# A PEER block kernel on one core: a new order of the build's steps, gate tiles with their own space, and the last 32 tokens' gates kept in SBUF

## Chip, cores and metric

One core of a Trainium2 chip runs the whole kernel. The metric is device time in microseconds (us) of one execution; lower is better. Engines are named as in the profile: PE is TensorE (its weight loads are PEld), DVE is VectorE, ACT is ScalarE, POOL is GpSimd, SP is SyncE, which here only issues DMAs.

## What is computed

Cut to the second half of the block, which the change touches (512 tokens, 1024 channels, 8 heads, 128 x 128 = 16384 experts, everything float32):

```python
def peer_ffn(h, w_q, sub_keys, expert_u, expert_v):
    q = (hb @ w_q).reshape(tokens, 8, 2, 128)
    s = einsum('thpc,hpkc->thpk', q, sub_keys)
    top_s, top_i = top_k(s, 16)                       # per head, for both halves of the key
    cand_s = top_s[:, :, 0, :, None] + top_s[:, :, 1, None, :]
    cand_i = top_i[:, :, 0, :, None] * 128 + top_i[:, :, 1, None, :]
    fin_s, fin_pos = top_k(cand_s, 16)                # 16 experts per token and head
    idx = take_along_axis(cand_i, fin_pos)
    gates = softmax(fin_s)
    act = gelu(einsum('thkd,td->thk', expert_u[idx], hb))
    return einsum('thk,thkd->td', gates * act, expert_v[idx])
# before it: a pooling and convolution mixer; after it: x + peer_ffn(h), and a final rmsnorm
```

## The kernel before, in words

Each token uses 128 of the 16384 experts. For the first 384 tokens (TD, three blocks of 128) the kernel does not fetch these experts' rows: it runs through all experts in 128 steps of 128 and multiplies with a dense matrix of gates that is zero nearly everywhere. For the last block of 128 tokens it gathers the rows of u and v by indirect DMA. Of the dense tokens the last 64 (TM) have their u products from gathered rows too, so the dense u product covers 320 tokens (TU).

float32 products are made of three matmuls on split operands: a high part (a cast by ACT) and a low part (raw minus high, a subtraction on DVE or POOL).

Stages, in the order of the program, all written out by hand (`manual_schedule`); every engine runs its instructions in that order, and so does each DMA queue:

- The mixer, up to some 290 us.
- **Norm and heads**: the normed tokens are transposed into h2H and h2L (`norm_T`), then for each head the queries, the keys' scores, and the best 16. Between these stand **u steps** (`u_tick`): step i loads a 128-expert block of u (`u_load`, two steps ahead of its cast), casts it (`u_high`, ACT), subtracts (`u_low`), multiplies it with the 320 tokens (`u_mm`, 24 matmuls), and applies Gelu (`u_act`, ACT), whose result is written to DRAM (Ad). n_ahead = 75 such steps are done ahead of the v stage: U_NORM at the norm, U_HEAD in the heads, U_GATE in the gates, 48 in the build, U_END after it.
- **Gates**: softmax, the keys' numbers (`pair_mults`, `pair_keys`), and three columns of 384 tokens (key 0, key 1, gate).
- **Build**: 48 pairs of two groups of four tokens. `one_hots(n)` makes two one-hot matrices oi and oj of 128 x 4 x 128 by compares on DVE; the gate is multiplied in either by four scalings on ACT (even groups) or in four 128-wide instructions on DVE that make oj (odd groups). Eight matmuls a pair set up the dense gate matrix of these tokens in PSUM; ACT copies it to `stage` (`to_stage`), and each 32 tokens' block goes to DRAM (Gd). Each pair also holds one u step. After each group `gather` uses and issues row gathers, by R_BUILD = 0.93 a group: 64 rows for the tokens of TM, then rows of the last block. `gather_use` is one DVE instruction a row (a dot product with a u row, or a multiply and add with a v row); after each 16 u rows of the last block ACT applies Gelu and POOL multiplies with the gates (L715, L716). Once the 64 rows are done, their dots go through a transpose on PE (L792) into the gate column.
- **v stage**: U_END = 4 u steps, then 128 v steps. Step i loads a block of v (`v_load`), splits it (`v_high`, `v_low`), loads gates from Gd (`g_load`, one gt tile for four steps) and Gelu values from Ad (`a_load`), multiplies them and splits the product into wH and wL (`weigh`), and runs 18 matmuls (`v_mm`). From step 74 on each step holds a u step too. The remaining gathers are spread evenly by PE's time per step (`cost`), to end seven steps before the last.

Row gathers have a ring of six buffers (GB = 6). All DMAs of loads go by SP's queue in program order, those of Ad and Gd by ACT's, gathers by POOL's. The tiles of gt and ab come from `epool`, which is set up after `opool` (one-hots) and `spool` (stage) are released, in their space.

## Time and profile before

| | before |
|---|---|
| time, median of 3 runs | 1572.73 us (1567.94 to 1572.83) |
| profiled execution, own time | 1573.27 us |
| its span | 1571.5 us |
| PE busy | 1483.9 us (94%) |
| DVE busy | 1241.7 us (79%) |
| ACT busy | 625.8 us (40%) |
| POOL busy | 715.7 us (46%) |
| HBM traffic | 266 GB/s over the span |

The share of busy time is a mean over stages with different limits, so it is read by stage. In the rows further down, a timeline row gives the start, the duration, engine and line, the operation with its tiles (out<-in) and shape, and in brackets the idle time of that engine before it and what ended it. Matmuls overlap, so the distance of two starts tells more than one's duration.

### The profile page before, as it was taken

To read this page: it belongs to the slowest core of one execution; us is meant where nothing else is said; L and a number is where in the kernel's file an instruction comes from. 1 tells how busy PE (TensorE), PEld (TensorE's weight loads), DVE (VectorE), ACT (ScalarE), POOL (GpSimd) and SP (SyncE) were. 2 spreads that over 40 slices of the span, in tenths; PEclk is the share of its full clock that TensorE was granted. 3 is DMA by queue.
4 is the path that set the end of the run, shared out by engine and by line. 5 is a ranking of instruction groups with operands and counts; after the bars stand their busy time and mean duration, and the time that the engine had idled before them with its cause. 6 is when DMAs were issued, how large, how long until landed. Compare 5 with 4: busy or idle time off the path is not lost. (4 is left out here: it accounts for less than half of the span.)

```text
span 1571.5 us, 22106 instructions
## 1 busy us (share of the span) xinstructions
PE 1483.9 (94%) x7953; PEld 1304.4 (83%) x7953; DVE 1241.7 (79%) x2455; ACT 625.8 (40%) x1016; POOL 715.7 (46%) x448
## 2 busy tenths in 40 slices
PE   8999999899997989888967999999999999999997
PEld 6788888788897988888966887887789999999996
DVE  6832334559999999999977888887788989898985
ACT  4222222433334555555542333333334333333344
POOL 3433222247777433333344444443355666566620
PEclk9999999999998999999998999999999999999999
DMA  5222234422224999999899999999999999999971
GB/s 181 88 87 82 92 108 161 153 92 107 80 93 140 346 337 374 333 366 381 324 392 350 342 358 338 360 352 319 332 366 336 370 378 361 374 364 356 360 282 67
DMA packets 167452, 419.57 MB, mean 267 GB/s; under 512 B 13744, under 2 KB 84144, under 8 KB 160688
## 3 DMA queue, kind: packets, MB, share of 16 engines
q1 hardware_dynamic: 106944, 212.92, 38.4%
q0 software_dynamic: 46144, 167.80, 28.2%
q10 hardware_dynamic: 14256, 37.46, 6.4%
q8 instruction: 62, 1.02, 0.2%
q14 instruction: 46, 0.38, 0.1%
HBM read 377.99 MB, written 39.55 MB: 266 GB/s over the span
## 5 line engine op out<-in xcount | busy, mean ns | idle before, releaser
L58 PE MATMUL b<-h2H,uH 128*128 128x320 f32 x1024 | 327.3, 320 | 29.8 <-ACT a L451 29.5
L60 PE MATMUL b<-h2H,uL 128*128 128x320 f32 x1024 | 321.2, 314 | 12.1 <-POOL uL L434 6.6
L59 PE MATMUL b<-h2L,uH 128*128 128x320 f32 x1024 | 321.0, 314 | 1.0 <-DVE h2L L55 1.0
L699 POOL DMA_INDIRECT gr<-in_expert_u,gidx x128 | 204.2, 1595 | 187.7 <-DVE dots L711 108.4
L699 POOL DMA_INDIRECT gr<-in_expert_v,gidx x128 | 189.8, 1483 | 144.9 <-DVE x L718 102.2
L864 PE MATMUL b<-vH,wH 128*128 128x512 f32 x768 | 242.0, 396 | 13.8 <-ACT wH L54 13.8
L864 PE MATMUL b<-vL,wH 128*128 128x512 f32 x768 | 239.2, 392 | 0.0
L864 PE MATMUL b<-vH,wL 128*128 128x512 f32 x768 | 239.0, 392 | 0.0
L58 PEld LDWEIGHTS b<-h2H,uH 128*128 128x128 f32 x1024 | 197.3, 193 | 36.6 <-ACT a L451 34.0
L60 PEld LDWEIGHTS b<-h2H,uL 128*128 128x128 f32 x1024 | 196.8, 192 | 13.0 <-POOL uL L434 6.8
L59 PEld LDWEIGHTS b<-h2L,uH 128*128 128x128 f32 x1024 | 197.0, 192 | 3.2 <-DVE h2L L55 1.2
L54 ACT CAST wH<-gt 128x384 fp32r<-128x384 f32 x128 | 65.7, 513 | 300.7 <-DVE gt L852 296.5
L864 PEld LDWEIGHTS b<-vH,wH 128*128 128x128 f32 x768 | 142.7, 190 | 44.9 <-ACT wH L54 19.7
L718 DVE SCALAR_TENSOR_TENSOR x<-gr,dots,x 128x1024 f32<-128x1024 f32 x128 | 164.0, 1281 | 15.0 <-DMA gr<-in_expert_v,gidx 13.2
L864 PEld LDWEIGHTS b<-vL,wH 128*128 128x128 f32 x768 | 145.5, 189 | 31.2
L864 PEld LDWEIGHTS b<-vH,wL 128*128 128x128 f32 x768 | 145.4, 189 | 30.7
L830 DVE TENSOR_TENSOR vL<-vr,vH 128x1024 fp32r<-128x1024 f32 x128 | 156.5, 1223 | 16.5 <-ACT vH L826 13.7
L826 ACT CAST vH<-vr 128x1024 fp32r<-128x1024 f32 x128 | 134.6, 1051 | 81.2 <-PE b L864 74.8
L711 DVE CUSTOM_DVE_ANT_0 gr<-gr,hn 128x1024 f32<-128x1024 f32 x128 | 152.3, 1219 | 9.2 <-DMA gr<-in_expert_u,gidx 9.1
L55 POOL TENSOR_TENSOR wl<-raw,wh 128x2048 fp32r<-128x2048 f32 (+1 forms) x21 | 79.3, 3775 | 156.0 <-ACT wh L54 156.0
L699 POOL DMA_INDIRECT gr<-in_expert_u,midx x64 | 82.4, 1288 | 124.9 <-DVE mdots L711 111.9
L430 ACT CAST uH<-ur 128x1024 fp32r<-128x1024 f32 x128 | 133.1, 1040 | 14.9 <-DMA ur<-in_expert_ut 9.4
(215 smaller groups left out, 2526.8 us busy)
## 6 DMA issues: line engine op xcount, KB each, us to landing
ur<-in_expert_ut SPq DMA_DIRECT2D x128, 512.0 KB, 7.1
vr<-in_expert_v SPq DMA_DIRECT2D x128, 512.0 KB, 6.7
Gd<-stage ACTq DMA_DIRECT2D x24, 1024.0 KB, 8.9
gt<-Gd SPq DMA_DIRECT2D x32, 768.0 KB, 10.0
raw<-in_w_in SPq DMA_DIRECT2D x15, 1024.0 KB, 4.8
Ad<-a ACTq DMA_DIRECT2D x75, 160.0 KB, 6.0
ab<-Ad SPq DMA_DIRECT2D x75, 160.0 KB, 7.9
raw<-in_w_q SPq DMA_DIRECT2D x8, 1024.0 KB, 8.7
```

The costliest lines, as they stand in the source:

```text
L54: nc.scalar.copy(Hd, src)
L55: (nc.gpsimd if pool else nc.vector).tensor_tensor(Ld, src, f(Hd), ALU.subtract)
L58: nc.tensor.matmul(o, lh, rh, start=first, stop=False)
L59: nc.tensor.matmul(o, lh, rl, start=False, stop=False)
L60: nc.tensor.matmul(o, ll, rh, start=False, stop=last)
L430: nc.scalar.copy(us[i][0], raws[i])
L699: nc.gpsimd.indirect_dma_start(out=r, out_offset=None, in_=io["expert_u" if kind == "u" else "expert_v"], in_offset=bass.IndirectOffsetOnA ...
L711: nc.vector.tensor_tensor_reduce(out=r, in0=r, in1=src, op0=ALU.mult, op1=ALU.add, scale=1.0, scalar=0.0, accum_out=dst)
L718: nc.vector.scalar_tensor_tensor(x1[:, KD + g], r, dots[:, g, k:k + 1], x1[:, KD + g], op0=ALU.mult, op1=ALU.add)
L826: nc.scalar.copy(vs[i][0], vraw[i])
L830: nc.vector.tensor_tensor(vs[i][1], vraw.pop(i), f(vs[i][0]), ALU.subtract)
L864: nc.tensor.matmul(acc[tb][hf], lw[:, ts], rw[:, hf * 512:(hf + 1) * 512], start=i == 0 and rw is vH and lw is wH, stop=last and i == NK - 1)
```

## The change

- The u steps: the second of U_NORM runs ahead of the last transpose, and U_GATE is 11 instead of 10, the added one ahead of the gates' key multiplications. n_ahead becomes 76.
- Order in a build pair: load and cast of the u block first, then the one-hots, and the u block's subtraction at the end, behind the gathers. Three of four groups (not two of four) have their gate multiplied in by ACT.
- Gathers in the build: 0.93 a group up to row 64, then R_LATE = 0.4 a group. In the four u steps after the build, two a step; before, in the first of them all that were issued.
- gt and ab have a pool of their own (`bpool`), so that their first loads stand in the build, four groups before its end. The two stage buffers lie in two pools, and the one with the last 32 tokens (`lpool`) stays to the end: that block is not written to Gd, and `g_rest` copies its part into each gt tile on ACT. gfin takes the space of hm.
- The gates' multiply of row dots is on DVE (after Gelu on ACT), four and eight rows after the chunk's last row in place of at once.

```diff
-U_NORM, U_HEAD, U_GATE, U_END = 2, (1, 1, 2, 1, 2, 1, 2, 1), 10, 4
+U_NORM, U_HEAD, U_GATE, U_END = 2, (1, 1, 2, 1, 2, 1, 2, 1), 11, 4
-R_BUILD = 0.93
+R_BUILD, R_LATE = 0.93, 0.4
...
-    Gd = dram.tile([TD // TG, P, NK, TG], F32, name="Gd")
+    Gd = dram.tile([TD // TG - 1, P, NK, TG], F32, name="Gd")
...
-    u_tick()
+    u_tick(U_NORM)
     norm_T(NT - 1, hn[:, 0], h2H, h2L, (bank(6), bank(7)))
-    u_tick(U_NORM - 1)
...
-    u_tick(2)
+    u_tick(3)
     pair_mults(H - 2)
...
-    u_tick(U_GATE - 5)
+    u_tick(U_GATE - 6)
...
                 if g is not None and k % CH == CH - 1:
-                    cs = slice(k - CH + 1, k + 1)
-                    nc.scalar.activation(dots[:, g, cs], dots[:, g, cs], AF.Gelu)
-                    nc.gpsimd.tensor_tensor(dots[:, g, cs], dots[:, g, cs], ggate[:, g, cs], ALU.mult)
+                    todo[n + 4] = todo[n + 8] = (g, slice(k - CH + 1, k + 1))
...
             n_done[0] += 1
+            if n in todo:
+                g, cs = todo.pop(n)
+                if n + 4 in todo:
+                    nc.scalar.activation(dots[:, g, cs], dots[:, g, cs], AF.Gelu)
+                else:
+                    nc.vector.tensor_tensor(dots[:, g, cs], dots[:, g, cs], ggate[:, g, cs], ALU.mult)
...
-    opool = tc.alloc_tile_pool(name="opool", bufs=3, reuse_waits="tile")
-    spool = tc.alloc_tile_pool(name="spool", bufs=2, side="right", reuse_waits="tile")
+    bpool = tc.alloc_tile_pool(name="bpool", bufs=2, reuse_waits="tile")
+    opool = tc.alloc_tile_pool(name="opool", bufs=4, reuse_waits="tile")
+    lpool = tc.alloc_tile_pool(name="lpool", bufs=1, side="right", reuse_waits="tile")
+    spool = tc.alloc_tile_pool(name="spool", bufs=1, side="right", reuse_waits="tile")
+    NG = TD // TG
...
-        if t1 + 4 == TG:
+        if t1 + 4 == TG and 4 * n // TG < NG - 1:
...
+    def g_rest(i):
+        if i < NK and i % IG == 0:
+            nc.scalar.copy(gt_of[i][:, NG - 1], stages[0][:, i:i + IG])
...
-        if n % 2 == 0:
+        if n % 4 != 3:
             compare(oj, cols[1])
...
-        one_hots(n + 2)
-        one_hots(n + 3)
         i = nu[0]
         nu[0] += 1
         u_load(i + 3)
         u_high(i + 2)
+        one_hots(n + 2)
+        one_hots(n + 3)
...
         u_act(i, u_mm(i))
-        u_low(i + 2, nc.vector)
+        if left == 4:
+            g_load(0)
+            a_load(0)
+            a_load(1)
...
-            gather(int((g + 1) * R_BUILD), 2)
+            gather(int(min((g + 1) * R_BUILD, TM + max(0, g + 1 - TM / R_BUILD) * R_LATE)), 2)
+        u_low(i + 2, nc.vector)
...
-    a_load(0)
-    a_load(1)
+    g_rest(0)
     for k in range(U_END):
         u_tick(1, nc.vector)
-        gather(n_issue[0], 2)
+        gather(n_done[0] + 2, 2)
...
         if k == 1:
-            g_load(0)
...
         g_load(i + 2)
+        g_rest(i + 2)
         a_load(i + 2)
```

On ACT, one pair of the build near its end (a Gd block is complete there). In the names, uH is the u block's high part, ur the loaded block, a the Gelu values, and the numbers tell one buffer from another. Before:

```order
L769 ACTIVATE oi<-oi,col_4159 128x128 x4
L430 CAST uH<-ur 128x1024
L745 COPY stage<-b_7213 128x128x4
L745 COPY stage<-b_7223 128x128x4
L749 DMA Gd<-stage 128x2048 x2
L451 ACTIVATE a<-b_7255 128x320
L453 DMA Ad<-a 128x320
```

The same pair of the changed kernel, and the one after it:

```order
L430 CAST uH<-ur 128x1024
L798 ACTIVATE oi<-oi,col_4193 128x128 x4
L753 COPY stage<-b_7248 128x128x4
L753 COPY stage<-b_7256 128x128x4
L757 DMA Gd<-stage 128x2048 x2
L451 ACTIVATE a<-b_7286 128x320
L453 DMA Ad<-a 128x320
L430 CAST uH<-ur 128x1024
L798 ACTIVATE oi<-oi,col_4193 128x128 x8
```

The cast stands ahead of the scalings, and every second pair has eight scalings instead of four.

On DVE, one pair of the build with two gathers (hm holds the tokens whose u products come from rows, mdots their dots, uL the u block's low part). Before:

```order
L762 TENSOR_TENSOR oi<-iota,col_4157 128x512
L762 TENSOR_TENSOR oj<-iota,col_4158 128x512
L762 TENSOR_TENSOR oi<-iota,col_4157 128x512
L773 TENSOR_SCALAR oj<-iota,col_4158,col_4159 128x128 x4
L434 TENSOR_TENSOR uL<-ur,uH 128x1024
L711 ISA gr,mdots<-gr,hm 128x1024
L711 ISA mdots 128x1
L711 ISA gr,mdots<-gr,hm 128x1024
L711 ISA mdots 128x1
```

The changed kernel, a pair of the other kind than the one with four L802 instructions, which stays in every second pair:

```order
L791 TENSOR_TENSOR oi<-iota,col_4191 128x512
L791 TENSOR_TENSOR oj<-iota,col_4192 128x512
L791 TENSOR_TENSOR oi<-iota,col_4191 128x512
L791 TENSOR_TENSOR oj<-iota,col_4192 128x512
L710 ISA gr,mdots<-gr,hm 128x1024
L710 ISA mdots 128x1
L710 ISA gr,mdots<-gr,hm 128x1024
L710 ISA mdots 128x1
L434 TENSOR_TENSOR uL<-ur,uH 128x1024
```

The four 128-wide instructions are one 512-wide compare in such a pair, and the subtraction has moved behind the gathers.

On SP, the loads from the build's last pairs into the v stage (ur: u blocks, ab: Gelu values, gt: gates, vr: v blocks). Before:

```order
L425 DMA ur<-in_expert_ut 128x1024 x11
L844 DMA ab<-Ad 128x320 x2
L425 DMA ur<-in_expert_ut 128x1024 x2
L836 DMA gt<-Gd 128x12x128
L425 DMA ur<-in_expert_ut 128x1024 x2
L916 DMA gfin<-in_g_final 128x1024
```

The changed kernel, from the same place:

```order
L425 DMA ur<-in_expert_ut 128x1024 x10
L765 DMA gt<-Gd 128x11x128
L778 DMA ab<-Ad 128x320 x2
L425 DMA ur<-in_expert_ut 128x1024 x5
L933 DMA gfin<-in_g_final 128x1024
```

The first gt load stands ahead of five u loads instead of two, and it reads eleven blocks instead of twelve.

## Rows read from the trace of the kernel before

**Rows 1.** Busy time by stage: stretch, length, each engine's busy us; PEclk, DMA share, GB/s.

```profile
508.00:800.00 292.00, 263.67 (x1907) 259.35 (x1905) 288.81 (x549) 165.05 (x375) 117.23 (x91) 0.98 0.95 352
800.00:850.00 50.00, 29.91 (x134) 25.78 (x134) 33.42 (x43) 15.66 (x25) 19.32 (x17) 0.80 1.02 387
855.00:1150.00 295.00, 289.03 (x1254) 235.35 (x1253) 239.24 (x318) 108.17 (x142) 126.74 (x78) 0.99 0.97 342
1160.00:1540.00 380.00, 380.00 (x2097) 344.42 (x2096) 332.73 (x408) 147.32 (x210) 211.51 (x139) 1.00 0.93 348
```

**Rows 2.** Timelines of PE, DVE and POOL around the last transpose: start, duration, instruction, [idle].

```profile
304.43 1.94 PE L166 MATMUL b<-ident,hn 128*128 128x128 f32 x8 [3.88 <-DVE hn L157]
...
311.25 0.39 PE L58 MATMUL b<-h2H,wh 128*128 128x512 f32 x1
...
298.16 2.12 DVE L146 TENSOR_TENSOR st<-st 128x1 f32<-128x1 f32 x1
...
307.02 0.69 DVE L55 TENSOR_TENSOR h2L<-b,h2H 128x512 fp32r<-128x512 f32 x1 [0.17 <-ACT h2H L54]
...
300.22 2.34 POOL L434 TENSOR_TENSOR uL<-ur,uH 128x1024 fp32r<-128x1024 f32 x1
```

**Rows 3.** Timelines of PE and POOL in the gates.

```profile
477.82 0.64 PE L60 MATMUL b<-h2H,uL 128*128 128x320 f32 x1 [6.57 <-POOL uL L434]
...
468.81 5.53 POOL L594 TENSOR_TENSOR eq<-eq,tf 128x1024 f32<-128x1024 f32 x2 [3.94 <-DVE eq L584]
```

**Rows 4.** Timeline of DVE over one pair of the build.

```profile
746.57 0.69 DVE L762 TENSOR_TENSOR oi<-iota,col 128x512 f32<-128x512 f32 x1
...
748.40 1.10 DVE L773 TENSOR_SCALAR oj<-iota,col,col 128x128 f32<-128x128 f32 x4
749.53 1.23 DVE L434 TENSOR_TENSOR uL<-ur,uH 128x1024 fp32r<-128x1024 f32 x1
750.68 1.22 DVE L711 CUSTOM_DVE_ANT_0 gr<-gr,hn 128x1024 f32<-128x1024 f32 x1
...
752.97 0.69 DVE L762 TENSOR_TENSOR oi<-iota,col 128x512 f32<-128x512 f32 x1
```

**Rows 5.** Timeline of PE in the build: build matmuls of the 34th and of later pairs.

```profile
710.67 1.98 PE L812 MATMUL b<-oi,oj 128*128 128x128 f32 x16
...
750.03 1.12 PE L792 MATMUL b<-ident,mdots 128*128 128x64 f32 x4 [5.51 <-ACT stage L745]
...
776.85 1.95 PE L812 MATMUL b<-oi,oj 128*128 128x128 f32 x16
...
782.15 1.95 PE L812 MATMUL b<-oi,oj 128*128 128x128 f32 x16
...
798.24 1.97 PE L812 MATMUL b<-oi,oj 128*128 128x128 f32 x16
```

**Rows 6.** Timelines of PE, SP, ACT and DVE between the build and the v stage.

```profile
850.14 0.62 PE L864 MATMUL b<-vH,wH 128*128 128x512 f32 x2
...
814.86 0.38 SPq L836 DMA_DIRECT2D gt<-Gd  x1
...
817.45 1.05 ACT L430 CAST uH<-ur 128x1024 fp32r<-128x1024 f32 x1 [8.54 <-DMA ur<-in_expert_ut]
...
816.92 1.23 DVE L711 CUSTOM_DVE_ANT_0 gr<-gr,hn 128x1024 f32<-128x1024 f32 x1 [3.61 <-DMA gr<-in_expert_u,gidx]
```

**Rows 7.** v stage: DVE timeline; waits (total, times, longest), 855:1150, 1160:1540; gathers' median landing.

```profile
1001.39 1.23 DVE L830 TENSOR_TENSOR vL<-vr,vH 128x1024 fp32r<-128x1024 f32 x1
...
1005.47 1.23 DVE L830 TENSOR_TENSOR vL<-vr,vH 128x1024 fp32r<-128x1024 f32 x1
...
PE b L864 <- ACT wH L54: 5.9, 9, 2.4
...
DVE wL L55 <- ACT wH L54: 29.0, 50, 0.6
...
gr<-in_expert_v,gidx POOLq DMA_INDIRECT x80, 8.3
```

More of the change, by code (lines that the diff above doesn't have):

```diff
@@ L373, in block_kernel @@
     hn = keep.tile([P, NT - KD, D], F32, name="hn")
-    hm = keep.tile([P, D], F32, name="hm") if TM else None
+    hm = keep.tile([P, D], F32, tag="hm", name="hm")
     h2H = keep.tile([P, DC, T], F32R, tag="hH", name="h2H")
@@ L690, in block_kernel @@
                 plan += [("v", g, k) for k in range((c - 1) * CH, c * CH)]
-    rows = {}
+    rows, todo = {}, {}
     n_issue, n_done = [0], [0]
@@ L742, in to_stage @@
         if t1 == 0:
-            stages[0] = spool.tile([P, NK, TG], F32, tag="stage", name="stage")
+            stages[0] = (lpool if (4 * n // TG) % 2 == (NG - 1) % 2 else spool).tile([P, NK, TG], F32, tag="stage", name="stage")
         stage = stages[0]
         nc.scalar.copy(stage[:, :, t1:t1 + 4], built.pop(n).rearrange("p (t i) -> p i t", t=4))
-        if t1 + 4 == TG:
+        if t1 + 4 == TG and 4 * n // TG < NG - 1:
             for q in range(2):
@@ L749, in to_stage, with g_load, a_load @@
                 nc.scalar.dma_start(Gd[4 * n // TG, :, ks], stage[:, ks])
+    gt_of = {}
+    def g_load(i):
+        if i < NK:
+            if i % IG == 0:
+                gt = bpool.tile([P, NG, IG, TG], F32, tag="gt", name="gt")
+                nc.sync.dma_start(gt[:, :NG - 1].rearrange("p n i t -> p n (i t)"),
+                                  Gd[:, :, i:i + IG, :].rearrange("n j i t -> j n (i t)"))
+                gt_of[i] = gt
+                for k in range(IG):
+                    gts[i + k] = gt[:, :, k]
+    def g_rest(i):
+        if i < NK and i % IG == 0:
+            nc.scalar.copy(gt_of[i][:, NG - 1], stages[0][:, i:i + IG])
+    def a_load(i):
+        if i < n_ahead:
+            abs_[i] = bpool.tile([P, TU], F32, tag="ab", name="ab", bufs=3)
+            nc.sync.dma_start(abs_[i], Ad[i])
     hot = {}
@@ L757, in one_hots @@
         tb, t0 = divmod(4 * n, P)
-        oi, oj = (opool.tile([P, 4, P], F32, tag=x, name=x, bufs=4) for x in ("oi", "oj"))
+        oi, oj = (opool.tile([P, 4, P], F32, tag=x, name=x) for x in ("oi", "oj"))
         full = [P, 4, P]
@@ L870, in v_mm @@
         del ws[i], vs[i]
-    gfin = epool.tile([P, D], F32, name="gfin", bufs=1)
+    gfin = keep.tile([P, D], F32, tag="hm", name="gfin")
     def add_acc(tb, hf):
@@ L972, in block_kernel @@
     epool.release()
+    bpool.release()
     vpool.release()
@@ L975, in block_kernel @@
     upool.release()
+    lpool.release()
 _SHAPES = {
```

12 lines of the change are left out of this document (removed).

## Prediction

> **What bounds the kernel now.** I read the table of stages first: TensorE's (PE) busy time against each stretch's length tells which stages can still give time. From 1160 to 1540, where every step does one step of both products (a u step and a v step), PE is busy all 380.00 us: nothing is to be had there except by doing less of it. From 855 to 1150 (v steps alone) 6.0 us of 295 are idle. The build, 508 to 800, has PE idle for 28.3 us of 292 while VectorE (DVE) is busy for 288.81 of them, so DVE sets its pace; and from 800 to 850 PE works for 29.9 us of 50 [rows 1]. Then I read the PE rows with idle time, stage by stage, and what released them: before the first query matmuls (3.88 us) [rows 2], in the gates (6.57) [rows 3], in the build [rows 5], and at the change from build to v stage [rows 6]. Last came the DVE rows of one build pair [rows 4] and of one v step [rows 7], for what a step needs at least.
>
> From these: 2097 matmuls at 42 a step are 49.9 steps in 380 us, 7.61 us each [rows 1]; a v step alone takes 4.08 (1005.47 less 1001.39) [rows 7], so a u step costs 3.53. A build pair needs 5.30 of PE where PE is never idle (782.15 less 776.85) [rows 5], and 6.40 of DVE with two gathered rows (752.97 less 746.57) [rows 4].
>
> **The change part by part**, against the profiled execution (span 1571.5, its own time 1573.27; the median of the runs shown is 1572.73, half a microsecond off, so one sum serves both).
>
> *Second u step ahead of the last transpose.* PE waits 3.88 us for hn, transposes, does a u step and begins the queries at 311.25 [rows 2]. With that u step in the wait, the queries wait only for the last h2L, which ended at 307.71 (307.02 plus 0.69): 3.5 us earlier, and 4.4 if the transposes run at full clock. One thing can eat this: a multiply of only 128x1 on DVE took 2.12 us beside GpSimd's (POOL) subtractions and ended, at 300.28, as the next of these began [rows 2]. The moved step's own subtraction on POOL (2.34 us in the row) falls where DVE makes hn, so up to 2.4 may be lost. I take -3, ends -4.4 and -1. The Trainium skill (SBUF — State Buffer, "SBUF: two separate sides") says that the port pair which VectorE and GpSimd share is a lock that one instruction keeps until it ends; the row agrees, and by that rule this term would be either -4 or -1.6, by who comes first, and nothing between.
>
> *One u step more in the gates (10 to 11).* POOL sat idle until the key multiplications at 468.81, and PE idle for 6.57 us until 477.82, behind those multiplications and one subtraction [rows 3]. The added tick's subtraction falls before 468.81, so PE does the step inside its wait: price 0 in the gates while this cover holds, 2.4 us if POOL starts the multiplications late. The v stage loses one u step: -3.5, ends -3.5 and 0.
>
> *Build, first 34 pairs.* In a DVE pair there are three 512-wide compares (0.61 each), four 128-wide ones (1.13 together, from 748.40 to 749.53), the u subtraction (1.15) and two gathers (2.29) [rows 4]. Every second pair now replaces the four by one 512-wide compare, -0.52, so -0.26 a pair. The first five pairs ran at PE's pace anyway: 29 x 0.26 = -7.5. The four scalings more fall to ScalarE (ACT), which is busy for 165 of 292 us [rows 1]. Casting before the scalings and subtracting after the gathers takes the cast off the way from compare to Gelu; it costs nothing while a load has two pairs to land. Ends -10 and 0 (0 if DMA, at 352 GB/s and 0.95 of its time, is the next bound).
>
> *Build, last 14 pairs.* Gathers drop from 1.86 to 0.8 a pair, so DVE needs 6.40 - 0.26 - 1.2 x 1.15 = 4.8 and PE's 5.30 bounds. Before, these pairs took from 710.67 to 800.21 (798.24 plus 1.97), 89.5 us [rows 5]. After: 14 x 5.30 + 1.95 = 76.2, plus what stays of the 5.51 us wait at 750.03, where the transposed dots wait for a bank that ACT empties. Before, PE made that wait good in the nine pairs after it; now nothing is there to catch up with, so it costs its full length. I take 3.5, since ACT comes closer to PE: 79.7, or -9.7. Ends -13 (no wait) and -5 (ACT bounds at some 5.6 us a pair: busy for 165 us in 48 pairs, 3.4 each, before two scalings more and issues that are not counted as busy).
>
> *From build to v stage.* Before, 800.21 to the third v step at 850.14: 49.9 us [rows 6]. The gt load left at 814.86, since its tile lay in the space of the build's tiles and its data ended with the last block; the u loads stood behind it on SP, and ACT waited 8.54 us for one. Now the gt and ab loads leave four pairs' blocks earlier, and the last 32 tokens come from SBUF by an ACT copy. What must run is 4 u steps and 2 v steps: 4 x 3.53 + 2 x 4.08 = 22.3. What is late next is DVE: from build end to the first weights it owes three subtractions, six gathers, two vL and the gate product, some 13.7 us, behind two block copies and a cast on ACT of 2.3: 16.0, against 14.1 of u steps; the second step is about 2 late the same way. With 2 more for matmuls at half clock after these waits, as from 800 to 850 (granted 0.80) [rows 1], 28.2: -21.5. Ends -27 and -10. POOL's multiply of a chunk of row dots, which held the gather queue behind it until ACT's Gelu, goes to DVE: eight instructions of 128x16, nothing on DVE, and the gathers behind it start earlier.
>
> *The v stage pays.* Before, 89 rows are done in the build and 10 in the four steps after it; now 74 and 8. So 238 of 320 are left in place of 221, 1.19 against 1.095 per v step and 3.24 against 2.98 where both run. A v step on DVE with one gather is full: 4.08 us with 0.1 idle [rows 7]. Each step with a second gather made PE wait for wH: 9 waits, 5.9 us [rows 7]. There will be seven more of these, 7 x 0.6 = 4, or by throughput (0.095 x 1.17 us x 75 steps) 8: I take +6. Where both run, DVE is busy 332.73 of 380 us and waits 29.0 for wH inside its step [rows 1, 7]: 7.25 of 7.61 per step; +0.26 x 1.17 makes 7.55, which just fits. For late landings +3. Together +9, ends 0 and +20. ACT's copy of a gate slice each fourth step hides: ACT is busy for 147 of 380 us.
>
> Sum: -3 - 3.5 - 7.5 - 9.7 - 21.5 + 9 = -36.2, so 1573.3 - 36.2 = **1537**.
>
> **The rivals.**
> 1. *The gather ring becomes the bound, and the kernel is slower.* Six buffers hold the rows, so a gather can be issued when the sixth before it has been used; the median landing is 8.3 us after its issue [rows 7]. At 2.98 rows a step six rows span 15.3 us, at 3.24 only 14.1, and POOL's three issues in a row take 4 to 6 of that. If the added reads lift landing over some 11 us, each step where both run waits for a row; at 1 us a step that is 46, so 1583. For it: DMA is busy 0.93 of the time already. Against: it moves 387 GB/s from 800 to 850, and 348 here [rows 1]. 0.06.
> 2. *The waits after the build were the gathers', not the tiles'.* DVE then still stands for rows at the end, half of the 27 us stays, and ACT bounds the last pairs: 1537 + 11.5 + 4.7 = 1553. For it: DVE stood there for rows, 3.61 us for one [rows 6]. Against: 387 GB/s were moved because blocks, gates and gathers all fell together, which the change pulls apart. 0.17.
> 3. *The new order buys nothing in the first 34 pairs, DMA being next*: 1537 + 7.5 = 1545. For it: 0.95 of DMA time. Against: 387 GB/s right after [rows 1]. 0.13.
> 4. *Everything at its good end*: -4.4 - 3.5 - 10 - 13 - 27 + 4 = -54, so 1519. It needs no wait at the transposed dots and none in the first v steps. 0.10.
>
> **How the numbers follow.** The forecast, 1537, has 0.50; rivals 1 to 4 have 0.06, 0.17, 0.13 and 0.10; 0.04 is left for no change. The forecast's own terms move it by some 8 either way. The range goes from rival 4 to just above rival 2 with its own spread: 1519 to 1560. Leaving out rival 1, no change and the outer part of rival 4, it holds about 0.85. 0.3% (4.7 us) is about the least that a measurement of this kernel tells from no change. Faster 0.90, same 0.04, slower 0.06.
>
> **What would show it.** Queries begin 2 to 4 us earlier; the gates' PE wait is near 3 us; build pairs take 5.8 and 6.4 in turn on DVE, then 5.3 on PE; PE idles at the transposed dots for 2 to 5 us; from build end to the third v step some 28 us pass; more short waits for wH stand in the v steps; DVE is busy for 92% or more where both run, with PE still full. It would be wrong if gathers land later than 11 us there, if ACT is busy throughout the last pairs, or if PE's waits after the build stay over 10 us.

## The result, and the profile after it

The changed kernel takes 1533.44 us (median of four runs, 1532.73 to 1536.65) where the kernel before, run beside it, took 1570.89: a ratio of 0.9767, 95% interval 0.9744 to 0.9791, or 37 us less, 33 to 40. The forecast was 1537. Its profiled execution took 1532.73 us with a span of 1531.0, against 1571.5 before, so 40.5 us have to be found in the trace.

The table by stage of the kernel after (stretch, length, busy us of each engine with its instructions, PEclk, DMA share, GB/s) answers to [rows 1]:

```profile
508.00:785.00 277.00, 264.82 (x1929) 257.54 (x1928) 262.56 (x456) 202.95 (x483) 123.83 (x80) 0.99 0.97 367
785.00:812.00 27.00, 24.15 (x131) 21.58 (x130) 22.75 (x33) 12.08 (x20) 14.83 (x9) 0.94 0.88 319
860.00:1100.00 240.00, 235.96 (x1028) 191.82 (x1027) 202.34 (x274) 92.03 (x133) 114.36 (x68) 1.00 1.00 355
...
1120.00:1500.00 380.00, 377.91 (x2084) 341.98 (x2084) 345.17 (x425) 149.54 (x223) 227.67 (x145) 1.00 0.96 359
```

The build lasts 277 us where it lasted 292, and DVE, busy for 288.81 of those, is now busy for 262.56 of these: it no longer holds PE in all of the build. The stretch between build and v stage shrank from 50 us at a granted clock of 0.80 to 27 at 0.94. In the steps where both products run, DVE's share rose from 332.73 of 380 us to 345.17, and PE has 2.1 us idle there where it had none.

The rows of PE after, around the last transpose, in the gates and ahead of the build (start, duration, instruction, [idle before it and what ended that]):

```profile
304.77 1.06 PE L166 MATMUL b<-ident,hn 128*128 128x128 f32 x8 [2.37 <-DVE hn L157]
306.07 0.80 PE L58 MATMUL b<-h2H,wh 128*128 128x512 f32 x1 [0.24 <-ACT h2H L54]
...
476.51 0.56 PE L60 MATMUL b<-h2H,uL 128*128 128x320 f32 x1 [5.17 <-POOL uL L434]
...
502.37 0.90 PE L645 MATMUL b<-ident,key 128*128 128x128 f32 x3 [4.99 <-DVE key L597]
503.50 0.90 PE L645 MATMUL b<-ident,key 128*128 128x128 f32 x3 [0.23 <-DVE key L597]
...
511.25 1.95 PE L844 MATMUL b<-oi,oj 128*128 128x128 f32 x16
```

The queries begin at 306.07, 5.2 us before [rows 2], but their first matmul takes 0.80 us, where one at full clock (that of 311.25 in [rows 2]) took 0.39: PE stood idle and ran transposes just before, and the granted clock from 304 to 312 is 0.79. Of the 5.2 us, 3.43 are left behind the queries, and stay so up to 462 us. Then DVE loses them. Its rows after, and those of POOL:

```profile
462.72 2.31 DVE L574 TENSOR_TENSOR dk<-thirty,dk 128x64 uint32<-128x64 uint32 x1
...
487.19 3.41 DVE L583 TENSOR_TENSOR eq<-af,rank 128x1024 f32<-128x1024 f32 x1
490.52 1.22 DVE L583 TENSOR_TENSOR eq<-dk,iota 128x1024 f32<-128x1024 uint32 x1
...
494.48 6.70 DVE L593 TENSOR_TENSOR eq<-eq,tf 128x1024 f32<-128x1024 f32 x2
```

```profile
462.54 2.41 POOL L434 TENSOR_TENSOR uL<-ur,uH 128x1024 fp32r<-128x1024 f32 x1 [1.13 <-ACT uH L430]
...
487.12 2.40 POOL L434 TENSOR_TENSOR uL<-ur,uH 128x1024 fp32r<-128x1024 f32 x1 [0.44 <-ACT uH L430]
490.64 3.37 POOL L434 TENSOR_TENSOR uL<-ur,uH 128x1024 fp32r<-128x1024 f32 x1 [1.12 <-ACT uH L430]
494.16 2.66 POOL L434 TENSOR_TENSOR uL<-ur,uH 128x1024 fp32r<-128x1024 f32 x1 [0.15 <-ACT uH L430]
497.68 2.42 POOL L434 TENSOR_TENSOR uL<-ur,uH 128x1024 fp32r<-128x1024 f32 x1 [0.85 <-ACT uH L430]
```

An operation of 64 columns starts at 462.72, 0.18 us behind a subtraction on POOL, and ends at 465.03, when that one has ended (462.54 + 2.41 = 464.95). The two pair multiplications took 6.70 us together (an operation of the same size takes 1.22 at 490.52, where DVE began ahead of POOL's next subtraction, and that one took 3.37). In the kernel before, they took 4.56:

```profile
495.92 4.56 DVE L594 TENSOR_TENSOR eq<-eq,tf 128x1024 f32<-128x1024 f32 x2
```

So the last keys come at 503.4, not earlier than before but 0.7 later; PE waits 5.2 us for them (two rows of L645), its next u step takes 4.80 us instead of 3.60 (the granted clock from 502 to 508 is 0.55, so part of it ran at the lower level), and the build's first matmuls stand at 511.25, where they stood at 508.79.

PE in and behind the build (pairs 38 to 40 and 48 of 48, the dots' transposes, and the first three v steps):

```profile
725.54 1.95 PE L844 MATMUL b<-oi,oj 128*128 128x128 f32 x16
730.84 1.95 PE L844 MATMUL b<-oi,oj 128*128 128x128 f32 x16
734.43 0.66 PE L821 MATMUL b<-ident,mdots 128*128 128x64 f32 x4 [1.64 <-ACT stage L753]
740.03 1.95 PE L844 MATMUL b<-oi,oj 128*128 128x128 f32 x16
...
782.48 1.95 PE L844 MATMUL b<-oi,oj 128*128 128x128 f32 x16
800.77 1.14 PE L883 MATMUL b<-vH,wH 128*128 128x512 f32 x2 [2.26 <-ACT wH L54]
...
807.35 0.73 PE L883 MATMUL b<-vH,wH 128*128 128x512 f32 x2 [0.59 <-ACT wH L54]
...
811.56 0.62 PE L883 MATMUL b<-vH,wH 128*128 128x512 f32 x2
```

A late pair takes 5.30 us (730.84 less 725.54). From the 39th to the 40th pair 9.19 us pass: 1.64 of waiting at the dots, and a u step that ran in part at the lower clock (granted 0.72 from 734 to 740). The build ends at 784.43 (782.48 + 1.95), and the third v step begins 27.1 us later, against 49.9 [rows 6].

Measured on PE's rows, the profiled executions compare like this (us; the build runs from its first matmuls to the end of its last):

| stage | before | after | difference |
|---|---|---|---|
| to the heads' first u step | 323.25 | 319.83 | -3.4 |
| from there to the build | 185.54 | 191.42 | +5.9 |
| build | 291.4 | 273.2 | -18.2 |
| build's end to third v step | 49.9 | 27.1 | -22.8 |
| third v step to the end | 721.4 | 719.4 | -2.0 |

The sum is -40.5, the whole difference of the spans.

### The profile page after: what moved, and what is told of

It is laid out like the page before. It is cut to its first block, busy times and chain, and to the rows that moved or that the text cites. A ratio compares the mean times of both kernels' runs of the same rounds, so it can differ in the third digit from the quotient of the medians.

```text
span 1531.0 us, 22164 instructions
## 1 busy us (share of the span) xinstructions
PE 1475.5 (96%) x7953; PEld 1291.9 (84%) x7953; DVE 1230.9 (80%) x2390; ACT 662.8 (43%) x1144; POOL 749.0 (49%) x441
## 4 chain that ended last, share of the span: by engine, by line
PE 47%; DVE 37%; issue 8%; ACT 4%; DMA 3%; POOL 0%; ACTq 0%; DVEq 0%; SPq 0%; POOLq 0%
PE b L883 19%; PE b L59 9%; PE b L58 9%; PE b L60 9%; DVE gr L710 6%; DVE vL L863 4%; DVE uL L434 4%; DVE x L715 3%; DVE oj L791 2%; ACT wH L54 2%; DVE oi L791 2%; DVE gt L871 1%; DVE eq L583 1%; DVE oj L802 1%; DVE key L597 1%
## 5 line engine op out<-in xcount | busy, mean ns | idle before, releaser
L60 PE MATMUL b<-h2H,uL 128*128 128x320 f32 x1024 | 321.0, 314 | 15.7 <-DVE uL L434 10.3
L58 PE MATMUL b<-h2H,uH 128*128 128x320 f32 x1024 | 323.3, 316 | 0.2 <-ACT h2H L54 0.2
L698 POOL DMA_INDIRECT gr<-in_expert_u,gidx x128 | 210.1, 1642 | 195.9 <-DVE dots L710 125.6
L698 POOL DMA_INDIRECT gr<-in_expert_v,gidx x128 | 204.0, 1594 | 161.8 <-DVE x L715 87.7
L60 PEld LDWEIGHTS b<-h2H,uL 128*128 128x128 f32 x1024 | 194.2, 190 | 23.1 <-DVE uL L434 17.6
L59 PEld LDWEIGHTS b<-h2L,uH 128*128 128x128 f32 x1024 | 194.3, 190 | 3.2 <-DVE h2L L55 1.2
L430 ACT CAST uH<-ur 128x1024 fp32r<-128x1024 f32 x128 | 133.9, 1047 | 36.0 <-ACT a L451 17.2
L698 POOL DMA_INDIRECT gr<-in_expert_u,midx x64 | 97.7, 1526 | 101.3 <-DVE mdots L710 83.4
```

Of the source, the lines that this page charges most:

```text
L58: nc.tensor.matmul(o, lh, rh, start=first, stop=False)
L59: nc.tensor.matmul(o, lh, rl, start=False, stop=False)
L60: nc.tensor.matmul(o, ll, rh, start=False, stop=last)
L430: nc.scalar.copy(us[i][0], raws[i])
L698: nc.gpsimd.indirect_dma_start(out=r, out_offset=None, in_=io["expert_u" if kind == "u" else "expert_v"], in_offset=bass.IndirectOffsetOnA ...
```

## The experiments

Each kernel is the changed one with an edit, unless it says otherwise. For all of them the same stages were read off PE's rows in the profiled execution; "pairs 1 to 34" runs from the start of the first pair's matmuls to that of the 34th's, and "39 to 40" is the step with the dots' transposes.

| kernel | first pair at | pairs 1 to 34 | 39 to 40 | build's end | to third v step | to the end | median |
|---|---|---|---|---|---|---|---|
| before | 508.8 | 201.9 | 13.0 | 800.2 | 49.9 | 721.4 | 1570.9 |
| after | 511.3 | 191.6 | 9.2 | 784.4 | 27.1 | 719.4 | 1533.4 |
| e1, ten steps in the gates | 505.1 | 193.7 | 13.5 | 784.6 | 28.1 | 720.7 | 1533.8 |
| e2, subtractions on DVE | 506.4 | 194.2 | 11.1 | 784.1 | 28.1 | 720.3 | 1534.1 |
| e3, old order in the build | 510.2 | 220.3 | 11.0 | 821.8 | 29.4 | 720.2 | 1573.3 |
| e4, rows late as before | 509.1 | 192.5 | 10.6 | 786.1 | 34.8 | 714.3 | 1537.5 |
| e5, half of the blocks scaled | 512.6 | 198.4 | 10.9 | 794.7 | 26.5 | 720.4 | 1537.0 |
| e6, gates' tiles at the old place | 509.6 | 192.1 | 9.8 | 783.9 | 36.1 | 719.9 | 1544.0 |
| e7, multiply on POOL | 506.7 | 193.7 | 11.5 | 784.2 | 28.0 | 742.9 | 1554.0 |
| e8, e2 and v loads late | 506.0 | 194.3 | 10.6 | 783.4 | 28.1 | 720.6 | 1532.8 |
| e9, before, multiply on DVE | 508.5 | 200.6 | 13.9 | 799.1 | 44.7 | 715.1 | 1559.7 |
| e10, e8 and another bank | 505.8 | 194.3 | 6.0 | 778.6 | 28.6 | 722.3 | 1529.7 |
| e11, e10 and fewer rows | 507.2 | 193.3 | 6.2 | 779.2 | 24.3 | 726.1 | 1531.3 |
| e12, e10 and more rows | 506.2 | 194.1 | 5.8 | 778.8 | 31.0 | 716.5 | 1529.6 |

### Where the start's gain went: e1 and e2

e1 takes the added u step out of the gates:

```diff
-U_NORM, U_HEAD, U_GATE, U_END = 2, (1, 1, 2, 1, 2, 1, 2, 1), 11, 4
+U_NORM, U_HEAD, U_GATE, U_END = 2, (1, 1, 2, 1, 2, 1, 2, 1), 10, 4
-    u_tick(3)
+    u_tick(2)
-    u_tick(U_GATE - 6)
+    u_tick(U_GATE - 5)
```

> Changed kernel with ten u steps in the gates again instead of eleven, everything else kept. In its profile the heads run 3.43 us earlier than before up to 462 us, but the first build matmuls come 2.5 later (511.25 against 508.79), since a 128x64 multiply on DVE took 2.31 us instead of 0.23 beside a subtraction of the added step on POOL, and three 128x1024 operations took 3.4 instead of 1.2. Theory A (the added step's subtractions on POOL hold up DVE, and DVE's keys set the build's start): without that step DVE and POOL meet as they did before the change, so the first build matmuls come at 508.8 - 3.4 = 505.4; the v stage has one u step more, 3.5; time 1533.4 - 5.9 + 3.5 = 1531. Theory B (the build's start is late for another reason, as the new order in the build): first build matmuls at 511, time 1533.4 + 3.5 = 1537.

e2 keeps the step, and leaves the last two subtractions to DVE:

```diff
-    u_tick(U_GATE - 6)
+    u_tick(U_GATE - 7)
+    u_tick(1, nc.vector)
...
-    u_tick(1, half=columns)
+    u_tick(1, nc.vector, half=columns)
```

> Changed kernel in which the last two u steps before the build leave their subtractions to DVE, behind the last keys, instead of POOL; eleven steps stay. Theory A (an operation of DVE that meets a subtraction of POOL is held until that ends): the two multiplications of pairs on DVE, 3.34 and 3.36 us in the changed kernel, take 1.2 each; the keys end 4.3 earlier, PE waits 1 to 2 us for them instead of 5.2 and does its next step at full clock (3.6 us, not 4.8); first build matmuls at about 506, time 1528. Theory B (these multiplications are slow by themselves, or what follows them sets the start): they stay at 3.4, two subtractions of 1.2 come on top, time 1534 to 1536.

Both did at the build's start what theory A said: first pair at 505.05 (505.4 expected) and 506.35 (506). One profile each would not be enough, since the start differs even among kernels whose code is the same up to the build: the changed one and e3 to e7 began it between 506.65 and 512.59, 509.9 on average. The five with e2's edit lie between 505.78 and 507.19, 506.3 on average, so e2's edit is worth some 3.6 us there, and the 511.25 of the changed kernel's profile is one of the later starts. DVE's rows of e2 show the two multiplications at 2.35 us together, where they took 6.70:

```profile
495.69 2.35 DVE L593 TENSOR_TENSOR eq<-eq,tf 128x1024 f32<-128x1024 f32 x2
497.97 2.33 DVE L597 TENSOR_REDUCE key<-eq 128x64 f32<-128x1024 f32 x2
500.22 2.34 DVE L434 TENSOR_TENSOR uL<-ur,uH 128x1024 fp32r<-128x1024 f32 x2
```

The time did not follow: 1533.77 us (ratio 0.9773, 0.9740 to 0.9807) and 1534.11 (0.9781, 0.9750 to 0.9813), against 0.9767 for the changed kernel. Nor did the u step that e1 gives back to the v stage cost the 3.5 us expected of it: from the third v step to the end e1 takes 720.7 us against 719.4. The table tells where the 5 to 6 us went. Some 2 to 3 of them are lost in the first 34 pairs, and the rest at the dots: the 40th pair stands at 740.03, 740.21 and 739.68 in the three kernels, whatever their start. This is e1 there:

```profile
726.75 1.95 PE L844 MATMUL b<-oi,oj 128*128 128x128 f32 x16
733.55 1.12 PE L821 MATMUL b<-ident,mdots 128*128 128x64 f32 x4 [4.84 <-ACT stage L753]
740.21 1.05 PE L844 MATMUL b<-oi,oj 128*128 128x128 f32 x8
```

### The build's edits: e3, e4, e5

e3 puts the steps of a pair back in their order:

```diff
+        one_hots(n + 2)
+        one_hots(n + 3)
         i = nu[0]
...
         u_high(i + 2)
-        one_hots(n + 2)
-        one_hots(n + 3)
...
         u_act(i, u_mm(i))
+        u_low(i + 2, nc.vector)
...
-        u_low(i + 2, nc.vector)
```

> Changed kernel with the order in the build's pairs as before: compares and scalings ahead of the load and the cast, the subtraction right behind the u step and ahead of the gathers; three of four blocks are still scaled on ACT. Theory A (the order is what lets DVE keep its pace): in every second pair the eight scalings (0.3 us each) stand ahead of the cast (1.03) on ACT, and DVE's subtraction stands behind both, so DVE waits about 1.3 + 1.0 - 0.6 = 1.7 us there in each of 17 such pairs among the first 34: 29 us, time 1560; in the last 14 pairs, where DVE has room, little more. Theory B (the order is worth nothing, the fewer and wider DVE instructions and fewer gathers are all): 1533, build 273 us long as in the changed kernel.

It measured 1573.25 us, ratio 1.0025 (1.0007 to 1.0043): one edit undone loses all that the change gained. The first 34 pairs are 28.8 us longer, the 29 of theory A; another 9.6 come in the last 14 pairs, where it expected little. The build lasts 311.6 us instead of 273.2. ACT and DVE in one pair of e3:

```profile
639.85 2.51 ACT L798 ACTIVATE oi<-oi,col 128x128 f32<-128x128 f32 x8 [2.89 <-DVE oi L791]
642.27 1.03 ACT L430 CAST uH<-ur 128x1024 fp32r<-128x1024 f32 x1
```

```profile
640.97 0.68 DVE L791 TENSOR_TENSOR oj<-iota,col 128x512 f32<-128x512 f32 x1
643.33 1.23 DVE L434 TENSOR_TENSOR uL<-ur,uH 128x1024 fp32r<-128x1024 f32 x1 [1.68 <-ACT uH L430]
```

The eight scalings stand ahead of the cast, the subtraction waits 1.68 us for it (1.7 expected), and the gathers stand behind the subtraction. The waits of e3 between 512 and 700 us (total, times, longest) show DVE standing for the cast, and PE standing in the same pairs, so the two do not add up:

```profile
DVE uL L434 <- ACT uH L430: 26.9, 15, 3.4
PE b L58 <- ACT a L451: 24.9, 19, 2.0
```

PE waits for a bank that Gelu empties, which comes late on ACT too. So with three of four blocks scaled on ACT the old order makes the build 20 us longer than before (311.6 against 291.4). e3 undoes two moves at once, the cast ahead of the scalings and the subtraction behind the gathers; no run separates them.

e4 keeps the rows late in the build:

```diff
-R_BUILD, R_LATE = 0.93, 0.4
+R_BUILD, R_LATE = 0.93, 0.93
```

> Changed kernel that uses 0.93 gathered rows a block throughout the build, as before, instead of 0.4 behind the first 64. In the changed kernel the last pairs of the build take 5.31 us, the pace of PE, against 6.05 (mean of 5.83 and 6.26) where DVE has nearly two rows a pair. Theory A, as the prediction priced it: 13 pairs x 0.74 = +9.6 in the build; in the v stage 15 rows fewer, -9 by the prediction's own term; time 1534, no change. Theory B, as the traces put it (from the third v step to the end the changed kernel is 2.0 us shorter, 3.5 of it the moved u step, so the rows cost 1.5 there): +9.6 - 1.5, time 1541 to 1542.

1537.49 us, ratio 0.9801 (0.9770 to 0.9831): 4 more, between A and B, and for neither's reasons. The build is 3.8 us longer (expected 9.6): the pairs behind the dots run at PE's pace all the same, as they did before the change; that the stop at the dots (10.6 us from pair to pair) lets DVE catch up fits this and was not tested by itself. The v stage is 5.1 shorter for 15 rows. And 7.7 us come between build and third v step, where ACT waited for the gates' load and for a u load:

```profile
791.21 1.08 ACT L753 COPY stage<-b 128x512 f32<-128x512 f32 x2 [4.49 <-DMA gt<-Gd]
795.39 1.04 ACT L430 CAST uH<-ur 128x1024 fp32r<-128x1024 f32 x1 [2.77 <-DMA ur<-in_expert_ut]
```

e5 scales every second block again:

```diff
-        if n % 4 != 3:
+        if n % 2 == 0:
```

> Changed kernel that scales every second block's one-hots on ACT again, not three of four; order and gathers as in the changed kernel. In it DVE does four 128-wide compares (1.12 us) for every second block again instead of every fourth. Theory A (DVE sets the pace of the first 34 pairs and nothing later gives it back): 0.52 us in every second pair, +7.5, time 1541. Theory B (what the first pairs gain or lose is absorbed at the transposed dots, as 4.1 us of an earlier start were in the two kernels with changed gates: the 40th pair came at 740.0 in the changed kernel, 740.2 and 739.7 in those): the wait there, 3.9 us longer than a pair's pace, vanishes first, so +3.6, time 1537.

1536.96 us, ratio 0.9791 (0.9772 to 0.9811), with single times from 1535.53 to 1543.31; the profiled execution was that last one. In it the first 34 pairs are 6.8 us longer, near the 7.5 of theory A, and nothing is absorbed at the dots; the other three are 2 to 4.5 us above the changed kernel, as theory B has it. How much of the 7 us reaches the end is left open.

### Between build and v stage, and the multiply: e6, e7, e9

e6 returns the gates' tiles to the space of the build's tiles, all of them by way of DRAM and loaded behind the build (the old `g_load`, and):

```diff
-        if left == 4:
-            g_load(0)
-            a_load(0)
-            a_load(1)
...
         if k == 1:
+            g_load(0)
...
-        g_rest(i + 2)
```

> Changed kernel with the gates' tiles in the space of the build's tiles again, all gates by way of DRAM and loaded behind the build; order, scalings and fewer late gathers kept. In the changed kernel 27.1 us pass from the build's end to the third v step, before 49.9; with 0.93 rows a block to the end and all else changed it was 34.8. Theory A (the tiles' home and the early load are most of this): 27.1 + 15 = 42, time 1548. Theory B (it was the crowd of gathers there, of which the fewer late gathers rid it, and the load's place only adds what one landing takes behind the build): 27.1 + 4 = 31, time 1537.

1543.97 us, ratio 0.9849 (0.9825 to 0.9872): 10.5 us more by the medians, between the two. From the build's end to the third v step 36.1 us pass, 9.0 more. The first v step waits in one piece for the gates, whose load left at 791.83 (SP, then PE):

```profile
791.83 0.38 SPq L843 DMA_DIRECT2D gt<-Gd  x1
```

```profile
808.87 1.22 PE L871 MATMUL b<-vH,wH 128*128 128x512 f32 x2 [10.88 <-ACT wH L54]
```

e7 puts the multiply of 16 row dots back on POOL:

```diff
-                    todo[n + 4] = todo[n + 8] = (g, slice(k - CH + 1, k + 1))
+                    cs = slice(k - CH + 1, k + 1)
+                    nc.scalar.activation(dots[:, g, cs], dots[:, g, cs], AF.Gelu)
+                    nc.gpsimd.tensor_tensor(dots[:, g, cs], dots[:, g, cs], ggate[:, g, cs], ALU.mult)
```

> Changed kernel with Gelu and gate multiply of 16 row dots right behind the sixteenth again, the multiply on POOL, where the gathers' issues stand behind it. The prediction put this edit at nothing that can be counted. Theory A (the later multiply on DVE gave the v stage some of what the additional gathers cost there): eight chunks, each holding the gather queue for some 1 us: +4 to +7, time 1537 to 1540. Theory B (it is hidden, since rows are issued four ahead): within 1 us, 1533.

Neither: 1553.97 us, ratio 0.9899 (0.9879 to 0.9919), 20.5 us lost by the edit that the prediction had put at nothing. It is all in the v stage, 742.9 us instead of 719.4. The waits of e7 from 812 us on:

```profile
POOL dots L715 <- ACT dots L714: 42.0, 7, 7.3
...
PE b L885 <- ACT wH L54: 23.3, 23, 6.9
...
DVE x L717 <- DMA gr<-in_expert_v,gidx: 16.4, 6, 4.8
```

POOL stands seven times, 6 us each, in its multiply until ACT has done Gelu, and the gathers behind it on POOL stand too; then a row is late, DVE waits 2.7 us a time for it, the weights behind that row on DVE are late, and PE waits 23.3 us for weights. In the changed kernel PE's wait in that stretch is

```profile
PE b L883 <- ACT wH L54: 7.5, 17, 1.1
```

The kernel before had the same stops of POOL, in the v stage and between build and v stage (its waits, 850 to 1571, and 785 to 850):

```profile
POOL dots L716 <- ACT dots L715: 40.3, 6, 10.4
```

```profile
POOL dots L716 <- ACT dots L715: 15.9, 1, 15.9
```

e9 asks what they cost there. It is the kernel before, with this one edit made:

```diff
-                    cs = slice(k - CH + 1, k + 1)
-                    nc.scalar.activation(dots[:, g, cs], dots[:, g, cs], AF.Gelu)
-                    nc.gpsimd.tensor_tensor(dots[:, g, cs], dots[:, g, cs], ggate[:, g, cs], ALU.mult)
+                    todo[n + 4] = todo[n + 8] = (g, slice(k - CH + 1, k + 1))
...
+            if n in todo:
+                g, cs = todo.pop(n)
+                if n + 4 in todo:
+                    nc.scalar.activation(dots[:, g, cs], dots[:, g, cs], AF.Gelu)
+                else:
+                    nc.vector.tensor_tensor(dots[:, g, cs], dots[:, g, cs], ggate[:, g, cs], ALU.mult)
```

> The kernel before with one edit alone: Gelu of 16 row dots four gathered rows later and their gate multiply on DVE another four later, instead of at once on POOL. In the changed kernel the same edit, undone, cost 20.5 us. From the third v step to the end the kernel before took 721.4 us with 221 rows left, one u step fewer makes 717.9; the changed kernel without late gathers saved, 223 rows left and the multiply on DVE, took 714.4. Theory A (the wait of POOL for Gelu costs time only where DVE has no room left to make it good, so it is the additional rows together with it): 717.9 - 714.4 = 3.5 faster, time 1569.2 - 3.5 = 1566. Theory B (the edit is worth its 20 us by itself): 1549.

1559.68 us, ratio 0.9930 (0.9904 to 0.9957): 11 us less, above A's 3.5 and below B's 20. By the table 6.3 us are saved in the v stage and 5.2 between build and v stage. So the edit is worth 6 us of the v stage with 221 rows left for it and 23 with 238; that DVE, which has less room with more rows, makes the difference fits theory A, but no run shows it by itself. The edit changes two things, when Gelu and the multiply are issued and which engine multiplies; no run separates these either.

### What holds PE at the dots: e8, e10

e8 is e2 with the first three v loads later:

```diff
-        if 24 <= left < 30:
-            v_load((28 - left) // 2)
+        if left in (16, 12, 8):
+            v_load((16 - left) // 4)
```

> The kernel with the last two subtractions ahead of the build on DVE, and in it the first three v loads (512 KB each) 16, 12 and 8 blocks ahead of the build's end instead of 28, 26 and 24. There the 38th and 39th pair came 2.3 us earlier than in the changed kernel, and the 40th only 0.35, since ACT waited 1.76 us for a u load that landed late, while 404 to 418 GB/s were moved and u loads took 8 to 10 us to land instead of 7.1. Theory A (the v loads are what delays the u loads at that place): the 40th pair comes 3 to 5 us earlier, the build's end too, time 1534 - 4 = 1530. Theory B (DMA is full in the whole build, so a delay moves to another place): build's end at 784 again, 1534. Theory C (the late v loads delay the gates' load or the first v step): end of the build earlier, the first v steps not, 1534.

1532.83 us, ratio 0.9765 (0.9746 to 0.9784). The 40th pair came at 739.00, the build's end at 783.40: 0.7 us better than e2, not 3 to 5. The v loads were not the cause. e10 changes the bank of the dots' transposes:

```diff
-            b = bank(2 + (n + 2) % 6)
+            b = bank(2 + n % 6)
```

> The kernel with the last two subtractions on DVE and late v loads, and in it the transposed dots written to a bank that ACT emptied a pair earlier (that of the pair's own first block) instead of the one of the next pair. Whatever the start of the build (505.1 to 511.3), the 40th pair came at 739.0 to 741.6 in seven kernels, since PE waits at the dots for ACT's block copy; here that wait was 3.07 us, and the step behind it ran at half clock. Theory A (only that bank holds PE there): no wait, the 40th pair 5.3 us behind the 39th, at 734, the build's end 5 earlier, time 1528. Theory B (ACT is a pair late there for other reasons, loads and issues while 404 to 418 GB/s are moved, and PE waits for it one step later): 40th pair at 739, time 1533.

```profile
728.10 1.95 PE L845 MATMUL b<-oi,oj 128*128 128x128 f32 x16
729.89 0.56 PE L822 MATMUL b<-ident,mdots 128*128 128x64 f32 x4
734.12 2.05 PE L845 MATMUL b<-oi,oj 128*128 128x128 f32 x16
```

These are PE's rows of e10. The wait is gone, the 40th pair comes 6.0 us behind the 39th, and the build ends at 778.63, 4.8 us before e8. Theory A holds for the place: the bank, which ACT empties a pair late, absorbed whatever had been gained before. Of these 4.8 us, 0.5 are lost on the way to the third v step and 1.7 behind it, and 1529.68 us remain, ratio 0.9742 (0.9713 to 0.9772). The 1.7 tell little: seven kernels with the same rows and steps in the v stage (the changed one, e2, e3, e5, e6, e8, e10) took 719.4 to 722.3 us for it.

### What a row costs behind the build: e11, e12

e11 takes one row instead of two in each of the four u steps behind the build, e12 takes 0.6 instead of 0.4 rows a block late in the build; both from e10.

```diff
-        gather(n_done[0] + 2, 2)
+        gather(n_done[0] + 1, 2)
```

> The same kernel with, in addition, one gathered row instead of two in each of the four u steps behind the build. DVE there owes three subtractions, rows, two vL and the gate product, and PE waits 1.6 and 2.2 us for the first two v steps' weights, both followed by half clock (5.8 us for the second v step instead of 4.1). Theory A (DVE is late there by these rows): 4 x 1.2 = 4.8 us less on DVE, no wait in the first v steps: 3.8 + 1.7 = 5.5 less there; four rows more in the v stage cost 5.1/15 each, 1.4: time 4 less than the kernel without. Theory B (ACT or the loads set the first weights): no less there, 1 more in the v stage.

```diff
-R_BUILD, R_LATE = 0.93, 0.4
+R_BUILD, R_LATE = 0.93, 0.6
```

> The kernel with subtractions on DVE, late v loads and the other bank for the dots, and in it 0.6 gathered rows a block instead of 0.4 behind the first 64: five or six rows more in the build, fewer in the v stage. Without that, DVE is busy for 45.27 us of the last 50 of the build (728 to 778) and DMA for 0.99 of them; from the third v step to the end 722.2 us pass, and four rows more made that 726.1. Theory A (rows in the v stage cost their time on DVE, some 1 us each, and the last pairs have room on DVE): 5 us less in the v stage, nothing in the build, time 1525. Theory B (DMA is full in the last pairs, so more rows there make loads late, as the fifteen rows of the kernel with 0.93 to the end, which cost 7.7 us between build and v stage): 3 more there, 2 to 5 less in the v stage, time 1528 to 1531.

e11: 1531.25 us, ratio 0.9755 (0.9729 to 0.9781). Between build and v stage 4.4 us less, as theory A said, but 3.9 more in the v stage for four rows, not 1.4. e12: 1529.63, ratio 0.9739 (0.9717 to 0.9762), six rows more in the build: 5.8 less in the v stage, as A said, 2.3 more between build and v stage, as B said; its profiled span is 3.3 us shorter than e10's, the medians are equal. The last 50 us of the build by engine, first e10, then e12:

```profile
728.00:778.00 50.00, 49.90 (x378) 49.63 (x377) 45.27 (x78) 40.84 (x98) 12.69 (x8) 1.00 0.99 362
```

```profile
728.00:778.00 50.00, 50.00 (x380) 49.89 (x379) 49.23 (x86) 37.95 (x93) 19.74 (x12) 1.00 1.01 386
```

PE keeps its pace in both; the rows that fall there, twelve instead of eight, fill DVE to 49.23 of 50 us. In the v stage a row cost about 1 us in e11 and e12 (3.9 for four, 5.8 for six), but 0.34 in e4 (5.1 for fifteen), and with the spread just named these prices are rough. Shifting rows moves time from stage to stage. e10 and e12 are the best versions found, 4 us (0.25%) below the changed kernel by their medians; the intervals of the three overlap, so this is a tendency and not a measured gain.

## Why the prediction came out right, point by point

**The total was right, and two of its parts were wrong in opposite directions.** Terms, as forecast and as the profiled executions show them: norm and gates -3 against +2.5; build -17.2 against -18.2; build to v stage -21.5 against -22.8; v stage +5.5 (+9, less 3.5 for the u step that leaves it) against -2.0. That an error of 5.5 us one way and one of 7.5 the other nearly cancel is luck.

**Norm, -3: right up to 462 us, and then gone.** -3.43 was measured, within the ends. The prediction saw that POOL's subtractions hold up DVE, and looked for it beside the norm, where it did not happen; it happened in the gates, where the added step's subtraction was priced at 0 "while this cover holds". PE's wait there, forecast at about 3 us, was 5.17. The step that failed is that cover: it asked who releases PE and not what DVE runs beside POOL. e1 and e2 show the cause by two ways; in e2 the same multiplications take 1.2 us each when POOL is silent. The Trainium skill (SBUF — State Buffer, "SBUF: two separate sides") calls the port pair that VectorE and GpSimd share a lock that is held for a whole instruction. The rows at 462.72 (2.31 us) and 494.48 (6.70 for two) agree.

**That this was lost did not matter much**, which the prediction had not foreseen either: e1, e2 and e7 began the build 4.6 to 6.2 us sooner than the changed kernel and ended it within 0.4 us of it. The wait at the transposed dots was forecast at 3.5 us as a cost of its own; it is one (9.19 us from pair to pair instead of 5.30, so 3.9), but it also swallows what comes early, since ACT, a pair late, sets its end. e10 shows that it was the choice of the bank.

**First 34 pairs, -7.5: the size was near (191.6 us against 201.9, -10.3, the good end), the reason was not.** The prediction took the gain from the wider compares and said of the order that it "costs nothing". e5's profiled execution, the slowest of its four, puts the compares at 6.8 us; e3 shows that without the order these pairs are 28.8 us longer than in the changed kernel. So the wider compares need the order. Whether the order also gains by itself is open: e5, with the new order and the old scalings, has these pairs 3.5 us shorter than before (198.4 against 201.9), but it began the build 3.8 us later, and a later start goes with shorter first pairs (193.7 in e7, which began at 506.7; 191.6 in the changed kernel, at 511.3).

**Last 14 pairs, -9.7:** from the 34th pair's matmuls to the end 81.6 us (784.43 less 702.82) against 89.5, so -7.9. With rows at the old rate (e4) they are only 2.9 us longer; the fewer rows a pair, the prediction's reason, show up behind the build instead. The stop at the dots, sized at 3.5, cost 3.9.

**Build to v stage, -21.5: right in size, and made of three things.** It was put down to the tiles' home and the early loads. Undone together, these two give 9.0 us (e6); the rows late in the build, undone alone, give 7.7 (e4); and the multiply, changed alone in the kernel before, gives 5.2 (e9). These come to 21.9 of 22.8, but that they add up is not shown: undone in the changed kernel (e7), the multiply gives only 0.9 there (28.0 against 27.1). Rival 2, that the waits were the gathers', was thus right for a third of it: the change takes the rows away there as well. Its price was too high by its own words, as half of the 27 us is 13.5, of which the forecast held 5.9 already: 1537 + 7.6 + 4.7 = 1549, not 1553. Rival 4 took +4 for the v stage, whose good end is 0. Neither touches the forecast.

**v stage, -3.5 and +9: the row's price was about right in e4, the multiply was left out, and the u step was not worth 3.5.** Fifteen rows cost 5.1 us (e4) with the multiply on DVE, where the prediction had +6 for seventeen; e11 and e12 have about 1 us a row. The u step put back (e1) costs 1.3 us there, which is no more than the spread of kernels with the same v stage; PE is idle for some 1.5 us less in e1 (720.7 less 706.2 busy, against 719.4 less 703.5). The prediction took PE's 3.53 us for the whole price of a step, though by its own sum DVE "just fits" there. The prediction saw that the multiply "held the gather queue behind it until ACT's Gelu", wrote "the gathers behind it start earlier", and gave that no number; in e9 it is worth 6.3 us in this stage, and with the added rows 23 (e7). Had these 6.3 us been counted, the forecast would have been 1531. Without the multiply's move, rival 1 would have come half true: the gathers late and PE waiting for weights, 743 us instead of 719, though by POOL's stops and not by slower landings, which rose only from 8.3 to 8.9 us:

```profile
gr<-in_expert_v,gidx POOLq DMA_INDIRECT x81, 8.9
```

**Rival 3** (DMA next in the first 34 pairs) is not borne out: they became 10.3 us shorter, with 0.97 of DMA time and 367 GB/s over the build against 0.95 and 352 before.

**What was to show it.** Build pairs of 5.83 and 6.26 in turn (5.8 and 6.4 forecast), then 5.30; 27.1 us to the third v step (28); 17 short waits for weights, 7.5 us from 812 on, against 9 waits and 5.9 us in [rows 7]; DVE at 91% where both run (92% forecast), with PE idle 2.1 us of 380 there and not full.

With e1's 1.3 us for the step the v stage's account closes: 721.4 less 1.3, less 6.3 for the multiply (e9), and 5.1 for the rows (e4) makes 718.9; 719.4 were measured. With 3.5 for the step it would be 716.7. Open stay what part of e5's loss in the first 34 pairs reaches the end, and what the order gains by itself.

## What to carry to other kernels

An instruction that waits on an in-order engine is priced by what is queued behind it: a multiply of 128x16 that waits for Gelu cost 11 us in one kernel and 20 in the other, because the gathers stood behind it. Edits that move work between engines are judged together with the order in which each engine gets it: here two more scaled blocks of eight shortened the first 34 pairs by 6.8 us in the new order (e5), while in the old order the build with them was 20 us longer than before (e3). And a u step moved out of the v stage gave at most some 1.3 us there, where its PE time is 3.5. Last, where a stage's end does not move although its start does, look for the wait in between that goes by something else, here a bank that was borrowed one pair too early.

## What the runs showed of the hardware

How DVE and POOL meet differs from one profiled execution to the next: six kernels with the same code up to the build began it between 506.65 and 512.59 us, and the five with the last subtractions on DVE between 505.78 and 507.19. Each kernel has one profile here, so how much one and the same kernel varies is not shown. Short operations are held up too: in the changed kernel a shift of 128x64 with two inputs from memory (the multiply of e1's expectation) took 2.31 us instead of 0.23 (462.72), and a shift by a constant, with one, 2.01 instead of 0.20 (481.53, begun 0.45 us behind a subtraction on POOL). The holding goes the other way too: the subtraction on POOL at 490.64, begun 0.12 us behind an operation of DVE, took 3.37 us instead of 2.40.
